# Retention, convolution and latent attention on one core: latent scaling inside the second query unit, and the shared key's columns beside the retention values

## The chip, the core and the metric

The kernel runs on one core of a Trainium2 chip. The metric is the device time of one execution in microseconds, lower is better. A profiled execution gives, beside its time, a trace: when each engine worked, on what, and what released it after each wait. The engines are TensorE (PE in the trace; its weight loads are PEld), VectorE (DVE), ScalarE (ACT), GpSimd (POOL) and the sequencer of SyncE (SP), which issues most of the DMA transfers.

## The reference, cut to what matters

x is 1024 rows of 1024 features in float32. All projections of x come from one matrix; the shared rope key is 64 of its columns, the query and key-value latents are 384 and 256 of them.

```python
h = rmsnorm(x, norm_g)
u_conv, u_ret, u_q, u_kv, u_kr, u_gate = split(h @ w_in)
y_conv = conv_module(u_conv, ...)        # GLU, 31 taps over the rows, channel LayerNorm, swish
y_ret = retention_branch(u_ret, ...)     # 4 heads of 128, rope, two scans, per-head norm
y_mla = mla_branch(u_q, u_kv, u_kr, ...) # latents are rms-normed, then 8 heads; k_rope = rope(u_kr)
y = concatenate([y_conv, y_ret, y_mla]) * silu(u_gate)
return rmsnorm(x + y @ w_out, final_g)
```

The rms norm of a latent is a division of each row of x's 1024 by that row's own root mean square, and a weight per latent channel.

## The kernel before

Everything is kept transposed: features lie on the 128 partitions, the 1024 rows of x along the free axis, in two halves of 512. A float32 product is made of three TensorE passes (`mm3`, L175 to L177) over high and low parts, so every operand is split once: ACT copies the high part (`xH`, `wh`), DVE subtracts to get the low part (`xL`, `wl`; L61 is the helper `stt` through which all such DVE operations go, L64 the helper `tt` for products and sums of two tensors on DVE or POOL).

The projections run as 21 units of 256 output columns (`run_unit`). A unit has four quarters (t = 0, 1 for the columns' halves, h = 0, 1 for the rows' halves) of 24 matmuls of 512 columns each. Units 0 to 3 feed the convolution, 4 to 7 are gates, 8 to 10 the latents, 11, 12 and 13 key, query and values of the first two retention heads, 14 a gate, 15 to 17 the other two heads, 18 to 20 gates. The values (`run_v`) are made the other way round, rows on the partitions, with 192 matmuls of 256 columns. Unit 10 holds one half of latent columns and one half in which the shared key's 64 columns stand twice.

Beside the units run background pieces (`bg`, `tick`). The convolution's taps are 120 DVE operations on 128 x 1024 (`acc <- hp, cwh, acc`); `hp` are the padded inputs of its four channel blocks. When the last tap of a block is done, the blocks are summed into `cm` (three DVE operations), TensorE sums `cm` over the channels (L353, two matmuls with a matrix of ones), DVE subtracts the mean, squares are summed into `va`, and so on to `y_dram`.

A latent quarter is evicted by DVE into `ca` (times the row factor of x's norm), stored to `l_dram`, squared by ACT, and the squares are added up by POOL in `lss` (query) and `lsk` (key-value). `row_rsqrt` (L300 to L308) sums these over the partitions on TensorE, in eight matmuls of one column for each of the two, and writes the 1024 row factors to `lq_dram` and `lk_dram`. After unit 20, when the attention begins, `lat` loads each half of a latent from `l_dram`, multiplies it by the broadcast row factors on DVE (ten products in all), and splits it; two more products make the shared key's rope parts (`kr`).

Rope of retention (`ev_rope`, L435 to L437): three DVE products of PSUM with tables, then one POOL sum into `k` or `q`.

TensorE's order, and that of each other engine, is fixed when the kernel is built, by the framework's scheduler; each engine then takes its queue in order and waits at the first instruction whose inputs are missing. At the start, `load_x` brings x in eight tiles of 128 features, SP issues, ACT scales by x's norm weights (in `vec`, one load of all small vectors issued by POOL), and TensorE runs warm-up passes (L264) on a zero tile. At the end, `finish` stores eight row blocks in two halves each, all issued by SP.

## Time and profile before

| | |
|---|---|
| median of three runs | 1117.38 us (1113.78 to 1118.88) |
| the profiled execution | 1115.57 us, span 1113.8 us |
| mean granted TensorE clock | 0.995 |
| TensorE busy | 1095.9 us, 98% of the span |
| DVE busy | 725.0 us, 65% |
| ACT busy | 412.9 us, 37% |
| POOL busy | 148.9 us, 13% |
| chain that ended last | TensorE 94%, DVE 3%, ACT 1%, DMA 1% |

The span runs from the first to the last instruction; the execution's own time is some 1.8 us longer. A granted clock of 1.00 is 2.4 GHz, the lower level 1.2 GHz; a figure between is a mean over a stretch with both.

### The profile page before, as it was taken

How to read it: one execution, taken by the hardware profiler on the slowest of the kernel's cores; microseconds unless marked ns; L12 is line 12 of the kernel's file. 1: busy time of each engine (PE TensorE's matmuls, PEld its weight loads, DVE VectorE, ACT ScalarE, POOL GpSimd, SP SyncE). 2: the span in 40 equal slices, each digit the busy share in tenths (PEclk: the TensorE clock that was granted, in tenths of full speed). 3: DMA queues.
4: the chain of work that ended last, by engine and by line, in shares of the span. 5: the costliest groups of instructions: out<-in, count | busy, mean ns of one | idle time of the engine just before them, and what ended most of it. 6: DMA issues, size and time to landing. Idle time of an engine off the chain costs nothing.

```text
span 1113.8 us, 14294 instructions
## 1 busy us (share of the span) xinstructions
PE 1095.9 (98%) x5568; PEld 920.2 (83%) x5568; DVE 725.0 (65%) x1011; ACT 412.9 (37%) x741; POOL 148.9 (13%) x135
## 2 busy tenths in 40 slices
PE   9999999999999999999899999999999999999997
PEld 7888888887898899888688888888888877888886
DVE  7599999998747694846865565655555572535033
ACT  8211221121144134324654554554554462424022
POOL 0200000213302442020201101200110000001000
PEclk9999999999999999999999999999999999999999
DMA  7221233221263121226211101211111241835112
GB/s 272 95 64 60 86 103 115 85 87 47 94 210 103 49 76 58 101 79 237 89 36 50 56 34 50 62 34 45 53 55 30 57 142 38 309 97 184 44 45 107
DMA packets 45620, 101.33 MB, mean 91 GB/s; under 512 B 5616, under 2 KB 9568, under 8 KB 45552
## 3 DMA queue, kind: packets, MB, share of 16 engines
q1 hardware_dynamic: 45504, 100.35, 27.2%
q8 instruction: 43, 0.70, 0.3%
q14 instruction: 25, 0.20, 0.1%
q0 software_dynamic: 48, 0.08, 0.0%
HBM read 74.14 MB, written 24.17 MB: 88 GB/s over the span
## 4 chain that ended last, share of the span: by engine, by line
PE 94%; DVE 3%; ACT 1%; DMA 1%; issue 1%; SPq 0%; POOLq 0%; POOL 0%; DVEq 0%; ACTq 0%
PE ps L175 24%; PE ps L176 24%; PE ps L177 24%; PE ps L831 5%; PE ps L813 3%; PE ps L817 3%; PE ps L816 3%; PE ps L814 3%; PE ps L815 3%; PE ps L576 1%; PE ps L565 1%; PE ps L300 1%; PE ps L580 1%; PE ps L578 1%; DMA xh<-lq_dram 0%
## 5 line engine op out<-in xcount | busy, mean ns | idle before, releaser
L176 PE MATMUL ps<-xL,wh 128*128 128x512 f32 (+1 forms) x612 | 238.9, 391 | 0.1
L177 PE MATMUL ps<-xH,wl 128*128 128x512 f32 (+1 forms) x612 | 238.6, 390 | 0.0
L175 PE MATMUL ps<-xH,wh 128*128 128x512 f32 (+1 forms) x612 | 236.3, 393 | 1.7 <-ACT xH L139 1.2
L61 DVE SCALAR_TENSOR_TENSOR acc<-hp,cwh,acc 128x1024 f32<-128x1024 f32 x120 | 154.0, 1323 | 0.1
L175 PEld LDWEIGHTS ps<-xH,wh 128*128 128x128 f32 x612 | 115.1, 189 | 25.5 <-ACT xH L139 1.4
L176 PEld LDWEIGHTS ps<-xL,wh 128*128 128x128 f32 x612 | 115.4, 188 | 24.2 <-DVE xL L61 0.8
L177 PEld LDWEIGHTS ps<-xH,wl 128*128 128x128 f32 x612 | 115.3, 188 | 23.8 <-issue 0.2
L61 DVE SCALAR_TENSOR_TENSOR PL<-ps,PH 128x512 fp32r<-128x512 f32 x128 | 85.6, 684 | 53.0 <-ACT PH L833 52.8
L833 ACT CAST PH<-ps 128x512 fp32r<-128x512 f32 x128 | 73.0, 588 | 92.2 <-PE ps L831 91.6
L176 PE MATMUL ps<-woL,yh 128*128 128x512 f32 (+1 forms) x264 | 100.8, 385 | 0.0
L177 PE MATMUL ps<-woH,yl 128*128 128x512 f32 (+1 forms) x264 | 100.2, 386 | 0.0
L175 PE MATMUL ps<-woH,yh 128*128 128x512 f32 (+1 forms) x264 | 100.0, 386 | 0.0
L820 DVE TENSOR_REDUCE nm<-ps 128x1 f32<-128x1024 f32 x64 | 78.1, 1220 | 31.9 <-PE ps L817 31.2
L166 ACT CAST wh<-wraw 128x1024 fp32r<-128x1024 f32 x40 | 42.1, 1052 | 126.0 <-PE ps L176 116.5
L822 ACT ACTIVATE P<-ps,nm 128x1024 f32<-128x1024 f32 x64 | 71.7, 1120 | 26.6 <-DVE nm L820 24.2
L831 PE MATMUL ps<-ident,P 128*128 128x128 f32 x512 | 72.8, 273 | 0.0
L831 PEld LDWEIGHTS ps<-ident,P 128*128 128x128 f32 x512 | 61.4, 140 | 12.7 <-DVE PL L61 0.8
L61 DVE SCALAR_TENSOR_TENSOR wl<-wraw,wh 128x1024 fp32r<-128x1024 f32 (+2 forms) x45 | 54.3, 1207 | 7.0 <-ACT wh L166 6.1
L813 PE MATMUL ps<-kH,qH 128*128 128x512 f32 x128 | 54.9, 429 | 3.8 <-DVE qL L61 2.6
L176 PEld LDWEIGHTS ps<-woL,yh 128*128 128x128 f32 x264 | 49.7, 188 | 10.3
L177 PEld LDWEIGHTS ps<-woH,yl 128*128 128x128 f32 x264 | 49.6, 188 | 10.2
L175 PEld LDWEIGHTS ps<-woH,yh 128*128 128x128 f32 x264 | 49.7, 188 | 10.0
(292 smaller groups left out, 1984.9 us busy)
## 6 DMA issues: line engine op xcount, KB each, us to landing
wraw<-in_w_in_dram SPq DMA_DIRECT2D x40, 512.0 KB, 3.5
wor<-in_w_out_dram SPq DMA_DIRECT2D x16, 512.0 KB, 4.7
g_dram<-ga SPq DMA_DIRECT2D x29, 256.0 KB, 2.2
yr<-y_dram SPq DMA_DIRECT2D x18, 256.0 KB, 3.7
g<-g_dram SPq DMA_DIRECT2D x16, 256.0 KB, 3.4
rb<-rs_dram SPq DMA_DIRECT2D x16, 256.0 KB, 3.1
y_dram<-osb SPq DMA_DIRECT2D x16, 256.0 KB
z<-in_x_dram SPq DMA_DIRECT2D x8, 512.0 KB, 3.5
```

Of the source, the lines that this page charges most:

```text
L61: eng.scalar_tensor_tensor(o, a, s, b, op0=op0, op1=op1)
L166: act.copy(hi, t)
L175: pe.matmul(o, sh, mh, start=first, stop=False, skip_group_check=skip)
L176: pe.matmul(o, sh, ml, start=False, stop=False, skip_group_check=skip)
L177: pe.matmul(o, sl, mh, start=False, stop=last, skip_group_check=skip)
L813: pe.matmul(o, qh[:, ts], kh, start=True, stop=False)
L814: pe.matmul(o, qh[:, ts], kl, start=False, stop=False)
L815: pe.matmul(o, ql[:, ts], kh, start=False, stop=False)
L820: dve.tensor_reduce(nm, self.S, axis=AX.X, op=MAX, negate=True)
L822: act.activation(p, self.S, AF.Exp, bias=nm, accum_out=self.rs[:, t:t + 1])
L831: pe.transpose(o[:, c * P:(c + 1) * P], self.p[t][:, (4 * j + c) * P:(4 * j + c + 1) * P], ident)
L833: act.copy(ph, o)
```

## The change

Four edits are made together.

1. Unit 10 runs its first half only. The shared key's 64 columns of weights are put beside the 256 of unit 13 (`load_v_kr`), whose matmuls become 320 wide (`run_v_kr`); ACT evicts values and key. After unit 14's first quarter `kr_rows` transposes the key's eight blocks on TensorE, multiplies by the rope tables on DVE and stores the two parts to `n_dram`, with sixteen transfers of 32 rows.
2. The latents are scaled in unit 12: `scale_lat`, called after each of its quarters, loads a whole latent tile and the row factors stay on chip in `lss` and `lsk`. POOL multiplies and the product goes to `n_dram`. The tiles have the tag `hp`, the convolution's inputs. `lat` then loads the scaled tile and only splits it, and the products and four row loads after unit 20 are gone.
3. x's norm weights come in a tile of their own (`gx`), loaded by SP second; `vec` is loaded by POOL at the very start. The first weight pieces are issued by ACT. The warm-up has nine rounds in place of twelve.
4. One of the last two stores is issued by ACT.

```diff
+WK = UW + 64
...
-NWARM = 12
+NWARM = 9
...
+    n_dram = [tc.dram_tile([P, S], F32, name=f"n_dram{i}") for i in range(QT + KVT + 1)]
...
+    gx = mk(const, [P, KT], tag="gx")
+    pool.dma_start(vec, vecs)
...
-        g = vec[:, V_G + k:V_G + k + 1]
+        g = gx[:, k:k + 1]
         for i in range(n):
             c = slice(i * S // n, (i + 1) * S // n)
             sp.dma_start(tf[:, c], xT[k * P:(k + 1) * P, c])
             if k == 0 and i == 0:
-                pool.dma_start(vec, vecs)
+                sp.dma_start(gx, vecs[:, V_G:V_G + KT])
                 w0[0][2](0, 1)
...
         def piece(a, b):
-            sp.dma_start(t[:, a:b], w_in[u, g, :, a:b])
+            (act if b == 1 or (g == 0 and b == 2) else sp).dma_start(t[:, a:b], w_in[u, g, :, a:b])
...
-    def run_unit(u, w, ev, nxt, per, hook=None):
+    def load_v_kr():
+        tiles = []
+        for tag in ("wh", "wl"):
+            two = [mk(p1, [P, 4, UW], F32R, tag=tag, bufs=4).rearrange("p a b -> p (a b)") for _ in range(2)]
+            two.append(mk(cv, [P, S + 2 * HALO], F32R, tag="hp", bufs=4))
+            tiles.append([v[:, :3 * WK].rearrange("p (a b) -> p a b", a=3) for v in two])
+        tk = mk(cv, [P, HS], tag="ca", bufs=4).rearrange("p (a b) -> p a b", a=KT)
+        for g in range(2):
+            sp.dma_start(tk[:, 4 * g:4 * g + 4], w_in[10, g, :, :, P:P + 64])
+        raw = []
+        for g in range(2):
+            raw.append(mk(p1, [P, 4, UW], tag="wraw", bufs=2))
+            sp.dma_start(raw[g], w_in[13, g])
+        for a, b in ((0, 3), (3, 4), (4, 6), (6, 8)):
+            for c, r in ((slice(0, UW), raw[a // 4][:, a % 4:a % 4 + b - a]), (slice(UW, WK), tk[:, a:b])):
+                hi, lo = (v[a // 3][:, a % 3:a % 3 + b - a, c] for v in tiles)
+                act.copy(hi, r)
+                split_l(dve, lo, r, hi)
+        return [(tiles[0][k // 3][:, k % 3], tiles[1][k // 3][:, k % 3]) for k in range(KT)]
+
+    def run_unit(u, w, ev, nxt, per, hook=None, each=None, ts=(0, 1)):
         res = None
-        for t in range(2):
+        for t in ts:
...
-                    res = load_unit(nxt)
+                    res = load_v_kr() if nxt == 13 else load_unit(nxt)
                 ev(t, h, o)
+                if each is not None:
+                    each(2 * t + h)
...
     for u in range(8, 11):
-        wn = run_unit(u, wn, ev_lat(2 * (u - 8)), u + 1, 2)
+        wn = run_unit(u, wn, ev_lat(2 * (u - 8)), u + 1, 2, ts=(0, 1) if u < 10 else (0,))
     lq_dram = tc.dram_tile([S], F32, name="lq_dram")
     lk_dram = tc.dram_tile([S], F32, name="lk_dram")
-    for ss, n, d in ((lss, 384.0, lq_dram), (lsk, 256.0, lk_dram)):
-        row_rsqrt(ss, 1.0 / n, EPS, None, d)
+    rows = []
+    for ss, n, d, tag in ((lss, 384.0, lq_dram, "lss"), (lsk, 256.0, lk_dram, "lsk")):
+        rows.append(mk(cv, [P, S], tag=tag))
+        row_rsqrt(ss, 1.0 / n, EPS, rows[-1], d)
+
+    def hp_tile():
+        return mk(cv, [P, S + 2 * HALO], tag="hp", bufs=4)
+
+    def scale_lat(i):
+        t = hp_tile()[:, :S]
+        sp.dma_start(t, l_dram[i])
+        if i < 5:
+            k = rows[int(i >= QT)]
+        else:
+            k = hp_tile()[:, :S]
+            sp.dma_start(k, t_mla[2])
+        tt(pool, t, t, k, MUL)
+        sp.dma_start(n_dram[i], t)
...
+    def run_v_kr(w, vN, per):
+        kn = mk(cv, [P, HS], tag="ca", bufs=4)
+        res = None
+        for st in range(NCH):
+            o = ps_main()
+            for k in range(KT):
+                mm3(o[:, :WK], xH[k][:, st * P:(st + 1) * P], xL[k][:, st * P:(st + 1) * P],
+                    w[k][0], w[k][1], k == 0, k == KT - 1)
+            if st == 0:
+                res = load_unit(14)
+            act.activation(vN[:, st, :], o[:, :UW], AF.Identity, scale=rcol[:, st:st + 1])
+            act.activation(kn[:, st * 64:(st + 1) * 64], o[:, UW:WK], AF.Identity, scale=rcol[:, st:st + 1])
+            if st % 2:
+                tick(per)
+        return res, kn
+
+    def kr_rows(kn):
+        for h in range(2):
+            o = ps_bg()
+            for j in range(4):
+                n = 4 * h + j
+                pe.transpose(o[:64, j * P:(j + 1) * P], kn[:, n * 64:(n + 1) * 64], ident)
+            tk, a = (hp_tile()[:64, :S].rearrange("p (c q) -> p c q", c=2) for _ in range(2))
+            hs = slice(h * HS, (h + 1) * HS)
+            for r, c, s0 in ((0, 0, 0), (32, 0, 32), (0, 1, 96), (32, 1, 64)):
+                sp.dma_start(tk[r:r + 32, c], t_mla[2][s0:s0 + 32, hs])
+            for c in range(2):
+                dve.tensor_tensor(a[:, c], o[:64], tk[:, c], op=MUL)
+            for r, c, s0 in ((0, 0, 0), (32, 0, 32), (0, 1, 96), (32, 1, 64)):
+                sp.dma_start(n_dram[5][s0:s0 + 32, hs], a[r:r + 32, c])
...
+    lat_at = {12: {0: (3, 4), 1: (0,), 2: (1,), 3: (2,)}}
     wn = run_unit(11, wn, ev_rope(kT[0], tr0, tmp0), 12, 3)
-    wn = run_unit(12, wn, ev_rope(qT[0], tr0, tmp0), 13, 3)
-    wn = run_v(13, wn, 14, vN[0], 3)
-    wn = run_unit(14, wn, ev_gate_t(8), 15, 6)
+    wn = run_unit(12, wn, ev_rope(qT[0], tr0, tmp0), 13, 3, each=lambda q: [scale_lat(i) for i in lat_at[12][q]])
+    wn, kn = run_v_kr(wn, vN[0], 3)
+    wn = run_unit(14, wn, ev_gate_t(8), 15, 6, lambda: kr_rows(kn))
...
-    def lat_rows(h):
-        rows[1, h] = row_bc(fin, "rb", lk_dram, h)
-        rows[0, h] = row_bc(wt, "xh", lq_dram, h)
...
-        sp.dma_start(t, l_dram[i][:, half(h)])
+        sp.dma_start(t, n_dram[i][:, half(h)])
         g = vec[:, V_QG + i:V_QG + i + 1]
-        tt(dve, t, t, rows[int(i >= QT), h], MUL)
         act.activation(lH[i][:, half(h)], t, AF.Identity, scale=g)
...
-        t, tk = mk(lx, [P, HS], tag="kr", bufs=2), mk(fin, [P, HS], tag="g" if h else "osb", bufs=2)
-        sp.dma_start(t, l_dram[5][:, half(h)])
-        sp.dma_start(tk, t_mla[2][:, half(h)])
-        tt(dve, t, t, tk, MUL)
+        t = mk(lx, [P, HS], tag="kr", bufs=2)
+        sp.dma_start(t, n_dram[5][:, half(h)])
         krt.append(t)
...
-            sp.dma_start(out[st * P:(st + 1) * P, half(c)], z[:, half(c)])
+            (act if st == 7 and c == 0 else sp).dma_start(out[st * P:(st + 1) * P, half(c)], z[:, half(c)])
```

Line numbers in the new kernel are a few higher (`tt` is L65, `stt` L62, `mm3` L179 to L181, the sums over the partitions L326, the cm matmul L379). The scheduler gives new orders in which the instructions stand.

POOL, from the end of unit 10 through unit 12, before (`k` and `q` are rope sums of units 11 and 12):

```order
L302 TENSOR_TENSOR rrc_1850<-rrc_1850,epsc_104 128x8
L302 TENSOR_TENSOR rrc_1866<-rrc_1866,epsc_104 128x8
L64 TENSOR_TENSOR k_1882<-ca_1928,ca_1929 128x512
L64 TENSOR_TENSOR k_1882<-ca_1962,ca_1963 128x512
L64 TENSOR_TENSOR k_1882<-ca_2001,ca_2002 128x512
L64 TENSOR_TENSOR k_1882<-ca_2042,ca_2043 128x512
L64 TENSOR_TENSOR q_1883<-ca_2095,ca_2096 128x512
L64 TENSOR_TENSOR q_1883<-ca_2149,ca_2150 128x512
```

And the same place now (`hp` are the latents that are scaled):

```order
L65 TENSOR_TENSOR k_1831<-ca_1911,ca_1912 128x512
L65 TENSOR_TENSOR k_1831<-ca_1945,ca_1946 128x512
L65 TENSOR_TENSOR hp_2059<-hp_2059,lsk_1813 128x1024
L65 TENSOR_TENSOR k_1831<-ca_1981,ca_1982 128x512
L65 TENSOR_TENSOR q_1832<-ca_2053,ca_2054 128x512
L65 TENSOR_TENSOR hp_2063<-hp_2063,lsk_1813 128x1024
L65 TENSOR_TENSOR hp_2106<-hp_2106,lss_1795 128x1024
L65 TENSOR_TENSOR q_1832<-ca_2100,ca_2101 128x512
L65 TENSOR_TENSOR hp_2166<-hp_2166,lss_1795 128x1024
L65 TENSOR_TENSOR hp_2212<-hp_2212,lss_1795 128x1024
```

Five products of twice the width stand among the rope sums of units 11 and 12.

TensorE at the end of unit 10 (`ps_1818` is its last quarter) and the start of unit 11, before:

```order
L176 MATMUL ps_1818<-xL_127,wh_1601 128x512
L177 MATMUL ps_1818<-xH_119,wl_1602 128x512
L300 MATMUL ps_1851<-ones_107,lss_1428 128x1 x8
L300 MATMUL ps_1867<-ones_107,lsk_1429 128x1 x8
L175 MATMUL ps_1891<-xH_112,wh_1735 128x512
```

And now:

```order
L180 MATMUL ps_1760<-xL_135,wh_1606 128x512
L181 MATMUL ps_1760<-xH_127,wl_1607 128x512
L326 MATMUL ps_1797<-ones_115,lss_1433 128x1 x8
L179 MATMUL ps_1840<-xH_120,wh_1740 128x512
L180 MATMUL ps_1840<-xL_128,wh_1740 128x512
L181 MATMUL ps_1840<-xH_120,wl_1741 128x512
L179 MATMUL ps_1840<-xH_121,wh_1740 128x512
L180 MATMUL ps_1840<-xL_129,wh_1740 128x512
L326 MATMUL ps_1815<-ones_115,lsk_1434 128x1 x4
L181 MATMUL ps_1840<-xH_121,wl_1741 128x512
```

The one-column sums of lsk have moved into unit 11, four of them here and four a quarter later.

TensorE at the convolution's sum over channels, before, in the third quarter of unit 11 (`ps_1976`):

```order
L175 MATMUL ps_1976<-xH_118,wh_1741 128x512
L353 MATMUL ps_1968<-cm_428,ones_107 128x512
L176 MATMUL ps_1976<-xL_126,wh_1741 128x512
L177 MATMUL ps_1976<-xH_118,wl_1742 128x512
L175 MATMUL ps_1976<-xH_119,wh_1741 128x512
L176 MATMUL ps_1976<-xL_127,wh_1741 128x512
L177 MATMUL ps_1976<-xH_119,wl_1742 128x512
L353 MATMUL ps_2015<-cm_428,ones_107 128x512
```

And now, in the third quarter of unit 12 (`ps_2135`):

```order
L179 MATMUL ps_2135<-xH_126,wh_1871 128x512
L180 MATMUL ps_2135<-xL_134,wh_1871 128x512
L379 MATMUL ps_1952<-cm_433,ones_115 128x512
L379 MATMUL ps_2067<-cm_433,ones_115 128x512
L181 MATMUL ps_2135<-xH_126,wl_1872 128x512
```

The two matmuls on cm stand four quarters of a unit further on in the row of units, twenty matmuls into a quarter.

## Rows read from the trace of the kernel before

**Rows 1.** The page's first part: busy time, share of the span, instructions.

```profile
PE 1095.9 (98%) x5568; PEld 920.2 (83%) x5568; DVE 725.0 (65%) x1011; ACT 412.9 (37%) x741; POOL 148.9 (13%) x135
```

**Rows 2.** Timeline of TensorE, units 10 and 13: start us, us, engine, line, out<-in.

```profile
225.29 0.39 PE L175 MATMUL ps<-xH,wh 128*128 128x512 f32 x1
...
230.73 0.39 PE L175 MATMUL ps<-xH,wh 128*128 128x512 f32 x1
...
302.76 0.28 PE L176 MATMUL ps<-wl,xH 128*128 128x256 f32 x1
...
308.52 0.28 PE L176 MATMUL ps<-wl,xH 128*128 128x256 f32 x1
```

**Rows 3.** Timeline of TensorE: one-column sums at the start and after unit 10.

```profile
36.32 1.84 PE L300 MATMUL ps<-ones,cm 128*128 128x1 f32 x16
...
249.10 1.84 PE L300 MATMUL ps<-ones,lss 128*128 128x1 f32 x16
250.80 1.93 PE L300 MATMUL ps<-ones,lsk 128*128 128x1 f32 x16
...
253.60 0.57 PE L176 MATMUL ps<-xL,wh 128*128 128x512 f32 x1
...
257.24 0.40 PE L176 MATMUL ps<-xL,wh 128*128 128x512 f32 x1
```

**Rows 4.** Windows: length; busy PE, PEld, DVE, ACT, POOL; PEclk; DMA share; GB/s.

```profile
38.00:43.00 5.00, 5.00 (x24) 4.14 (x24) 0.91 (x6) 0.00 (x0) 1.67 (x1) 1.00 0.03 10
253.00:258.00 5.00, 5.00 (x17) 3.91 (x16) 4.96 (x7) 0.00 (x0) 4.33 (x2) 0.66 0.47 157
```

**Rows 5.** Timeline of TensorE, start; in brackets idle before, and its releaser.

```profile
9.91 1.20 PE L175 MATMUL ps<-xH,wh 128*128 128x512 f32 x4 [1.18 <-ACT xH L139]
```

**Rows 6.** Windows, the attention's first tiles.

```profile
525.00:545.00 20.00, 15.85 (x62) 10.88 (x61) 18.04 (x30) 12.36 (x23) 3.84 (x3) 0.91 0.50 172
```

**Rows 7.** Timeline of TensorE, the attention's first scores.

```profile
539.92 0.50 PE L813 MATMUL ps<-kH,qH 128*128 128x512 f32 x1 [2.62 <-DVE qL L61]
```

**Rows 8.** Groups of DVE from 511 to 545: busy us, mean ns | idle before.

```profile
L64 DVE TENSOR_TENSOR lt<-lt,xh 128x512 f32<-128x512 f32 x4 | 2.6, 682 | 0.0
```

**Rows 9.** Timeline of SP's issues, the rotated query.

```profile
535.40 2.50 SPq L762 DMA_DIRECT2D xs<-xr  x4
```

**Rows 10.** Timeline of the last microseconds, SP's issues.

```profile
1110.01 0.81 SPq L1046 DMA_DIRECT2D out_dram<-z  x2
```

**Rows 11.** Timeline of DVE, from unit 10 to unit 15.

```profile
234.15 4.70 DVE L61 SCALAR_TENSOR_TENSOR acc<-hp,cwh,acc 128x1024 f32<-128x1024 f32 x3
...
245.79 2.47 DVE L61 SCALAR_TENSOR_TENSOR acc<-hp,cwh,acc 128x1024 f32<-128x1024 f32 x2
...
260.04 0.69 DVE L435 TENSOR_TENSOR ca<-ps,xn 128x512 f32<-128x512 f32 x1 [0.21 <-POOL rrc L302]
...
262.17 2.41 DVE L61 SCALAR_TENSOR_TENSOR acc<-hp,cwh,acc 128x1024 f32<-128x1024 f32 x1
264.61 1.22 DVE L64 TENSOR_TENSOR cm<-cm,acc 128x1024 f32<-128x1024 f32 x1
...
287.79 2.38 DVE L64 TENSOR_TENSOR va<-va,cb 128x512 f32<-128x512 f32 x2
...
343.22 0.15 DVE L507 TENSOR_SCALAR kd<-kd 128x8 f32<-128x8 f32 x1
```

**Rows 12.** Timeline of POOL: the rope tables, and a sum of unit 11.

```profile
49.92 4.79 POOL L64 TENSOR_TENSOR xn<-xn,rbc 128x1024 f32<-128x1024 f32 x2 [9.73 <-DMA rbc<-r_dram]
...
262.21 1.28 POOL L64 TENSOR_TENSOR k<-ca,ca 128x512 f32<-128x512 f32 x1 [2.20 <-DVE ca L437]
```

**Rows 13.** Timeline of TensorE: cm, va, the first decayed values' product.

```profile
269.79 1.02 PE L353 MATMUL ps<-cm,ones 128*128 128x512 f32 x2
...
291.33 0.95 PE L300 MATMUL ps<-ones,va 128*128 128x1 f32 x8
...
353.82 0.23 PE L175 MATMUL ps<-w,w 128*128 128x128 f32 x1
```

More of the change, by code (lines that the diff above doesn't have):

```diff
@@ L105, in body @@
     pool.memset(eps_c, -0.5)
-    cwh = mk(const, [P, 144], tag="cwh")[:, :NC_CONV * CONV_K]
+    cwh = mk(const, [P, 136], tag="cwh")[:, :NC_CONV * CONV_K]
     ones = mk(const, [P, P], tag="ones")
@@ L403, in ev @@
             sp.dma_start(l_dram[i][:, hs], a)
-            if i < 5:
-                dst = lss if i < QT else lsk
-                if i in (0, QT):
-                    act.activation(dst[:, hs], a, AF.Square)
-                else:
-                    sq = mk(cv, [P, HS], tag="cb", bufs=2)
-                    act.activation(sq, a, AF.Square)
-                    tt(pool, dst[:, hs], dst[:, hs], sq, ADD)
+            dst = lss if i < QT else lsk
+            if i in (0, QT):
+                act.activation(dst[:, hs], a, AF.Square)
+            else:
+                sq = mk(cv, [P, HS], tag="cb", bufs=2)
+                act.activation(sq, a, AF.Square)
+                tt(pool, dst[:, hs], dst[:, hs], sq, ADD)
         return ev
     for u in range(8, 11):
-        wn = run_unit(u, wn, ev_lat(2 * (u - 8)), u + 1, 2)
+        wn = run_unit(u, wn, ev_lat(2 * (u - 8)), u + 1, 2, ts=(0, 1) if u < 10 else (0,))
     lq_dram = tc.dram_tile([S], F32, name="lq_dram")
     lk_dram = tc.dram_tile([S], F32, name="lk_dram")
-    for ss, n, d in ((lss, 384.0, lq_dram), (lsk, 256.0, lk_dram)):
-        row_rsqrt(ss, 1.0 / n, EPS, None, d)
+    rows = []
[9 more added lines that the diff above has]
+            k = rows[int(i >= QT)]
+        else:
+            k = hp_tile()[:, :S]
+            sp.dma_start(k, t_mla[2])
+        tt(pool, t, t, k, MUL)
+        sp.dma_start(n_dram[i], t)
     def trig(pl, tag):
@@ L663, in half @@
         return slice(i * HS, (i + 1) * HS)
-    def row_bc(pl, tag, d, h):
-        t = mk(pl, [P, HS], tag=tag)
-        sp.dma_start(t, d[half(h)].rearrange("(o s) -> o s", o=1).to_broadcast([P, HS]))
-        return t
-    krt, rows = [], {}
-    def lat_rows(h):
-        rows[1, h] = row_bc(fin, "rb", lk_dram, h)
-        rows[0, h] = row_bc(wt, "xh", lq_dram, h)
+    krt = []
     def lat(i, h):
@@ L686, in body @@
     LT = [(lx, "lt", LTB)] * LTB + [(fin, "osb", 2), (fin, "g", 2)] * 2
-    lat_rows(0)
     lat(3, 0)
@@ L866, in body @@
     g_r(0, 0)
-    lat_rows(1)
     lat(3, 1)
```

## Prediction

> **What bounds the kernel now.** I read the engines' busy times first: TensorE is busy for 98% of the span [rows 1], so time can only go in three ways: fewer or narrower matmuls, fewer waits of TensorE, or less time at the lower clock. Then I read TensorE's timeline for the price of a matmul. Two starts 24 matmuls of 512 columns apart differ by 5.44 us, or 0.2267 us each; two starts 48 matmuls of 256 columns apart differ by 5.76 us, or 0.120 us each [rows 2]. A straight line through both gives 0.0133 us plus 0.000417 us a column, hence 0.1467 us for 320 columns, a width that the trace does not have. Last I looked for the stretches in which TensorE waits or runs slow near the lines touched: the sums of squares after unit 10, the attention's first tiles, the start, and the end.
>
> **The change part by part.**
>
> *Matmuls.* Unit 10's second half held 48 matmuls of 512 columns: 48 x 0.2267 = 10.9 us go. Unit 13's 192 matmuls grow from 256 to 320 columns: 192 x 0.0267 = 5.1 us come. Eight transposes come, each no dearer than a 256-column matmul: at most 1.0 us, I take 0.9. Net **-4.9**, all of it on the path, since TensorE is the path. Bounds: if the 320-column step costs as a 512-column one in proportion (0.142) or has the line's offset twice (0.160), the net moves from -5.8 to -2.3.
>
> *The clock after the sums.* Before, 16 one-column passes for lss and 16 for lsk stand together [rows 3]. Behind them nine intervals of 512-column matmuls take 3.64 us instead of 2.04, and the granted clock of that stretch is 0.66, which is 1.2 GHz for a part of it and 2.4 GHz for the rest [rows 3, 4]. Behind the one set of 16 at 36.32 the clock stays at 1.00 [rows 3, 4]. The change puts six full matmuls after lss, and splits lsk in two. I take the whole dip as gone, **-1.6** (0 to -1.6).
>
> *Start.* TensorE waits 1.18 us for the first 512-column x tile at 9.91 [rows 5]. The norm weights now come in a small load of their own, and two weight pieces are issued by ACT; but the bytes ahead of that tile are the same. I take **-0.4** (0 to -1.2). Three fewer rounds of warm-up cost nothing unless the clock falls there: the real matmuls follow within the same microseconds.
>
> *Attention's first tiles.* In 525 to 545 us TensorE is busy for 15.85 of 20, so 4.15 are idle, and the mean granted clock is 0.91 [rows 6]: 20 x 0.09 = 1.8 us more at 1.2 GHz. Some 6 us are to be had. The biggest wait, 2.62 us, is for qL of DVE [rows 7], and DVE is full there: 18.0 of 20 us [rows 6]. The change takes ten products of 0.68 us for the latents (four of them are in [rows 8]) and two for the key off DVE, about 8 us, and six loads of 256 KB. What stays is the chain of the rotated query: four small copies issued one after another in 2.50 us [rows 9] and three POOL products behind. So not all 6 come back: I take **-4** (-2 to -6).
>
> *End.* One of the two last stores, which SP issues in 0.81 us [rows 10], goes to ACT: **-0.3** (0 to -0.4). These gains make -11.2.
>
> *The price: conv's end on DVE.* The scaling now stands in unit 12 as five POOL products of 128x1024, and conv's last taps lie there too. What POOL does to DVE the trace shows: two taps alone take 2.47 us, one beside POOL's k product (1.28 us long) 2.41 [rows 11, 12]. So a 512-wide POOL product costs DVE about 1.2 us where DVE has two SBUF inputs, and a 1024-wide one, 2.4 us long [rows 12], about 2.4. The Trainium skill, "GPSIMD Engine Reference", section 1 (Specifications), says that POOL's SBUF interfaces are shared with VectorE and collide with DVE instructions of two SBUF inputs, and section 4.1 sends elementwise tile work to VectorE. By that rule the products give DVE nothing back, and the time is the forecast's; were the ports separate, it would be the first rival's. The 2.41 us row agrees with the rule.
>
> DVE works from 234.15 without a real gap until cm is done at 264.61 + 1.22 = 265.8 [rows 11]: 31.7 us. TensorE asks for cm at 269.79 [rows 13], 4 us later. In the new order the same stretch ends four quarters further on, two of them in place of the two that unit 10 lost. It loses two evictions of 0.7 (-1.4), and gains four more rope groups of 2.1 each (the one from 260.04 to 262.17 [rows 11]; +8.5), the weight splits for unit 13 (two of 1.2 and small ones; +3.2), four more rope products of POOL beside taps or splits (4 x 1.2 = +4.8), and one or two scalings on POOL (+2.4 to +4.8). That makes 49.2 to 51.6 us, so cm is done at 283.4 to 285.8. TensorE gets there sooner: unit 10 ends one half (10.9) before 249.1, at 238.2; then the sums 3.5, unit 11 21.8, and 15.4 into unit 12: about 279.0. The wait is 4.4 to 6.8; some products will meet DVE on PSUM inputs, which costs nothing, so I take **+5** (0 to +9, the latter with a third scaling ahead of cm). The matmuls behind it stand in TensorE's one queue and all wait. A wait that long is followed in this trace by the lower clock (the 2.62 us wait lies in the stretch of 0.91 [rows 6, 7]): **+1.7** (0 to 2).
>
> *What cm passes on.* The squares' sums (va) come next. DVE's last va products end at 287.79 + 2.38 = 290.2, and TensorE's matmul is at 291.33 [rows 11, 13], 1.2 us of margin; between cm and va DVE gets more in its way than TensorE does: **+1** (0 to 3.8). Then the tail: kd is ready at 343.37 [rows 11], 52.0 us after that va matmul, and one ACT product and one split later the first matmul on it could start, some 53.3; it is at 353.82 [rows 13], 62.5 after. In the new order fewer matmuls stand between the two (144 of 512, 122 of 320 instead of 167 of 512, 192 of 256): about 53. The margin of 9 is spent to zero: **+1** (0 to 9, from sixteen more small copies on SP at 2.50/4 = 0.6 each).
>
> Sum: -4.9 - 1.6 - 0.4 - 4 - 0.3 + 5 + 1.7 + 1 + 1 = **-2.5** against the profiled execution's 1115.57: 1113.1. The median shown, 1117.38, is 1.8 higher, the lowest run 1.8 lower; I go a little up from the sum, to 1113.5. A measurement of this kernel tells about 0.5% (5.6 us) from no change.
>
> **The rivals.**
>
> *No wait at cm.* POOL's products fall beside rope, whose inputs are in PSUM, and DVE keeps its 42.0 us without contention: cm is ready at 234.15 + 42.0 = 276.2 + what k products add, at most 279. Then only the gains stand: 1115.57 - 11.2 = 1104.4. For it: TensorE's order was given a place for cm well behind DVE's bare work. Against it: the 2.41 us tap.
>
> *The latents' gain is small.* If the copies for the rotated query and their POOL products set the time by themselves, the wait for qL is only renamed, and -4 becomes -1: 1116. Against it: the copies start from DVE's rows, which come earlier with 8 us taken off.
>
> *The tail blocks (slower).* The sixteen copies of 32 rows go on SP's queue between the loads and stores of conv's normalisation, and the tables for the next heads wait for that tail. If all sixteen stand ahead, 16 x 0.6 = 9.6 us, the first product with the decayed values waits about 9 instead of 1, with 1.7 of slow clock behind it: 1113.1 + 8 + 1.7 = 1122.8. It decides from the point where the tail grows by more than the zero margin above; under 4 us it stays inside my range. For it: SP's queue is in order. Against it: half of the copies are behind the stores that matter, or DMA is nearly idle there.
>
> *The change does not separate the sums.* If the lower clock follows anyway and the five 1024-wide products cost nothing more, 1115.1: inside the forecast's range.
>
> **How the numbers follow.** Forecast, a wait at cm of some 5 us: 0.44, between 1109 and 1118. No wait: 0.30, 1102 to 1107. Small gain at the latents: 0.10. Tail: 0.10. Clock unchanged: 0.06. The range must reach to the no-wait case and short of the tail: 1103 to 1121. Faster by over 0.5%: the 0.30 and a quarter of the forecast, 0.41. Slower: the tail and a little of the small-gain case, 0.12. Within 0.5%: the rest, 0.47.
>
> **What would show it.** In the changed kernel's profile: starts of unit 13's matmuls 0.147 apart; no stretch at half clock behind lss; taps of over 2 us beside POOL's hp products; an idle of 4 to 7 us of TensorE before the cm matmuls, released by DVE's cm, and the lower clock behind it; in the attention's first 20 us no wait for qL and less than 2 us idle; the first product with kd with a wait near zero. I am wrong if cm is there before TensorE (then 1104), if the idle near the latents stays at 4, or if the first matmul on the decayed values waits more than 4 us.

## The result

The changed kernel takes 1124.53 us (median of 6 runs, 1122.53 to 1126.21), the kernel before 1118.01 us beside it (1113.78 to 1119.00): a ratio of 1.0068, 95% interval 1.0051 to 1.0086. It is slower by 6.5 us between the medians and 7.6 by the ratio. The prediction was 1113.5, with a range to 1121 and a chance of 0.12 for this side. One later execution, of the kernel `ends`, took 1916.6 us at a mean granted clock of 0.67 and is left out of that kernel's ratio.

The page of the profiled execution (1126.21 us, span 1124.4, the slowest of the six) shows at once where to look: TensorE's busy time is that of [rows 1], but the chain that ended last, TensorE's for 94% before, is now TensorE's for 83% only.

```profile
PE 1095.6 (97%) x5522; PEld 920.4 (82%) x5522; DVE 729.8 (65%) x1007; ACT 415.4 (37%) x755; POOL 165.3 (15%) x140
...
PE 83%; DVE 8%; DMA 4%; issue 3%; ACT 1%; SPq 0%; POOL 0%; POOLq 0%; DVEq 0%; ACTq 0%
```

TensorE's timeline gives the waits (in brackets: idle before, released by). "The decayed values" are the retention values times the decay factors kd, in unit 15; the first matmul on them reads the tiles `w,w`. A later `w,w`, in unit 17, waits too. These waits and those for cm and va are new; that for qL has shrunk from [rows 7], and one for QA, the rotated query, has come.

```profile
281.94 3.39 PE L379 MATMUL ps<-cm,ones 128*128 128x512 f32 x4 [2.85 <-DVE cm L65]
...
301.90 1.02 PE L326 MATMUL ps<-ones,va 128*128 128x1 f32 x8 [1.11 <-DVE va L65]
...
361.03 0.48 PE L179 MATMUL ps<-w,w 128*128 128x128 f32 x1 [4.48 <-ACT w L608]
...
420.61 0.39 PE L180 MATMUL ps<-w,w 128*128 128x256 f32 x1 [1.82 <-DVE w L62]
...
547.89 0.50 PE L873 MATMUL ps<-kH,qH 128*128 128x512 f32 x1 [0.96 <-DVE qL L62]
...
553.85 0.50 PE L876 MATMUL ps<-K,QA 128*128 128x512 f32 x1 [2.00 <-ACT QA L835]
```

Behind these waits the granted clock (third number from the end) is low for a while. 5 us at 0.66 lose 1.7 us, 25 us at 0.86 lose 3.5, and 25 us at 0.93 lose 1.75.

```profile
280.00:285.00 5.00, 3.06 (x5) 1.44 (x5) 4.81 (x6) 0.22 (x1) 5.00 (x3) 0.66 0.35 112
350.00:375.00 25.00, 20.52 (x97) 17.38 (x97) 22.05 (x51) 8.34 (x24) 10.41 (x7) 0.86 0.20 72
400.00:425.00 25.00, 23.18 (x146) 21.28 (x145) 24.40 (x44) 7.87 (x17) 11.43 (x9) 0.93 0.21 65
550.00:575.00 25.00, 23.00 (x116) 19.06 (x115) 15.47 (x21) 15.29 (x28) 6.17 (x5) 0.93 0.11 28
```

From one same matmul in both, 581.91 before and 592.07 after, the two profiles are 10.2 us apart, and at the end 10.6, so nearly all of it happens earlier. The parts: start -0.4, matmuls -4.9, the dip of [rows 3] -1.6, cm 2.85 and its clock 1.7, va 1.1, the decayed values 4.5 and their clock 3.5, the later `w,w` 1.8 and its clock 1.75. That is +10.3; the attention's first tiles gave nothing in this execution (before, 4.15 idle and 1.8 of clock; after, waits of 1.32, 0.96 and 2.00 us and 1.75 of clock: some 6.0 each).

```profile
581.91 0.50 PE L175 MATMUL ps<-lH,whk 128*128 128x512 f32 x1 [1.01 <-DVE kL L61]
```

```profile
592.07 0.50 PE L179 MATMUL ps<-lH,whk 128*128 128x512 f32 x1 [1.01 <-DVE kL L62]
```

Two causes for the lateness offered themselves. The first is POOL's products beside DVE. In the changed kernel's DVE and POOL timelines a weight split of 768 columns takes 3.15 us beside a product of 2.86, and later one of 1024 columns 3.44 beside two that take 6.06 (an operation of that width on two SBUF inputs takes 1.22 in [rows 11]):

```profile
265.86 3.15 DVE L62 SCALAR_TENSOR_TENSOR wl<-wraw,wh 128x768 fp32r<-128x768 f32 x1
...
291.57 3.44 DVE L62 SCALAR_TENSOR_TENSOR wl<-wraw,wh 128x1024 fp32r<-128x1024 f32 x1
```

```profile
265.32 2.86 POOL L65 TENSOR_TENSOR hp<-hp,lsk 128x1024 f32<-128x1024 f32 x1 [0.47 <-DMA lsk<-lk_dram]
...
291.21 6.06 POOL L65 TENSOR_TENSOR hp<-hp,lss 128x1024 f32<-128x1024 f32 x2 [3.52 <-DMA hp<-l_dram]
```

The second is the transfers behind unit 14. Followed back from the wait at 361.03, the chain (start, us, what) runs through loads, one of which takes 7.05 us and one 6.76, with two issues of the small stores (L532) in between:

```profile
320.66 4.80 DMA cb<-g_dram
...
329.51 7.05 DMA cb<-g_dram
...
337.70 3.90 DMA cb<-g_dram
...
343.53 0.45 SPq L532
344.02 0.54 SPq L532
...
345.91 6.76 DMA w<-in_t_idx_dram
```

### The profile page after: what moved, and what is told of

Same layout as the page of the kernel before. It is cut to its first block, busy times and chain, and to the rows that moved or that the text cites. A ratio compares the mean times of both kernels' runs of the same rounds, so it can differ in the third digit from the quotient of the medians.

```text
span 1124.4 us, 14278 instructions
## 1 busy us (share of the span) xinstructions
PE 1095.6 (97%) x5522; PEld 920.4 (82%) x5522; DVE 729.8 (65%) x1007; ACT 415.4 (37%) x755; POOL 165.3 (15%) x140
## 4 chain that ended last, share of the span: by engine, by line
PE 83%; DVE 8%; DMA 4%; issue 3%; ACT 1%; SPq 0%; POOL 0%; POOLq 0%; DVEq 0%; ACTq 0%
PE ps L179 20%; PE ps L180 20%; PE ps L181 20%; PE ps L891 4%; PE ps L873 3%; PE ps L876 3%; PE ps L877 3%; PE ps L874 3%; PE ps L875 3%; DMA cb<-g_dram 1%; DVE acc L62 1%; DVE w L62 1%; DMA g_dram<-xr 1%; DVE wl L62 1%; PE ps L649 1%
## 5 line engine op out<-in xcount | busy, mean ns | idle before, releaser
L180 PE MATMUL ps<-xL,wh 128*128 128x512 f32 (+1 forms) x596 | 232.0, 390 | 0.6 <-DVE xL L62 0.5
L181 PE MATMUL ps<-xH,wl 128*128 128x512 f32 (+1 forms) x596 | 232.4, 391 | 0.0
L179 PE MATMUL ps<-xH,wh 128*128 128x512 f32 (+1 forms) x596 | 229.3, 392 | 2.8 <-DVE xr L62 1.3
L62 DVE SCALAR_TENSOR_TENSOR acc<-hp,cwh,acc 128x1024 f32<-128x1024 f32 x120 | 154.3, 1324 | 0.1
L179 PEld LDWEIGHTS ps<-xH,wh 128*128 128x128 f32 x596 | 111.8, 188 | 26.1 <-DVE xr L62 1.7
L180 PEld LDWEIGHTS ps<-xL,wh 128*128 128x128 f32 x596 | 112.3, 188 | 23.5 <-DVE xL L62 1.2
L181 PEld LDWEIGHTS ps<-xH,wl 128*128 128x128 f32 x596 | 112.3, 188 | 23.3 <-issue 0.5
L62 DVE SCALAR_TENSOR_TENSOR PL<-ps,PH 128x512 fp32r<-128x512 f32 x128 | 85.5, 685 | 52.3 <-ACT PH L893 52.2
L181 PE MATMUL ps<-woH,yl 128*128 128x512 f32 (+1 forms) x264 | 100.2, 386 | 0.0
L179 PE MATMUL ps<-woH,yh 128*128 128x512 f32 (+1 forms) x264 | 100.0, 386 | 0.0
L170 ACT CAST wh<-wraw 128x1024 fp32r<-128x1024 f32 x38 | 39.8, 1052 | 107.2 <-PE ps L180 99.8
L62 DVE SCALAR_TENSOR_TENSOR wl<-wraw,wh 128x1024 fp32r<-128x1024 f32 (+3 forms) x46 | 60.9, 1327 | 4.8 <-ACT wh L170 4.7
L65 POOL TENSOR_TENSOR g<-g,rb 128x512 f32<-128x512 f32 x16 | 21.0, 1314 | 254.7 <-DMA rb<-rs_dram 209.5
L180 PEld LDWEIGHTS ps<-woL,yh 128*128 128x128 f32 x264 | 49.7, 188 | 10.2
L179 PEld LDWEIGHTS ps<-woH,yh 128*128 128x128 f32 x264 | 49.7, 188 | 10.1
L181 PEld LDWEIGHTS ps<-woH,yl 128*128 128x128 f32 x264 | 49.6, 188 | 10.1
```

The lines of the kernel that those rows point to most:

```text
L62: eng.scalar_tensor_tensor(o, a, s, b, op0=op0, op1=op1)
L170: act.copy(hi, t)
L179: pe.matmul(o, sh, mh, start=first, stop=False, skip_group_check=skip)
L180: pe.matmul(o, sh, ml, start=False, stop=False, skip_group_check=skip)
L181: pe.matmul(o, sl, mh, start=False, stop=last, skip_group_check=skip)
```

## The experiments

Theory A says that both causes act, on a way that the shared key's new place has made shorter for TensorE; B, that POOL's products cause all; C, that the shorter way alone does. Ratios are to the kernel before, run beside each; an expectation in microseconds that was written against another session's median is judged by the ratio.

| kernel | median us | before beside it | ratio (95%) |
|---|---|---|---|
| no_scale | 1119.26 | 1115.44 | 1.0029 (1.0014 to 1.0044) |
| no_merge | 1113.94 | 1115.44 | 0.9984 (0.9970 to 0.9997) |
| thin_products | 1116.26 | 1115.44 | 1.0015 (0.9993 to 1.0037) |
| few_copies | 1120.74 | 1115.44 | 1.0037 (1.0016 to 1.0057) |
| wide_key | 1118.23 | 1115.28 | 1.0020 (0.9997 to 1.0043) |
| late_wide | 1128.80 | 1115.28 | 1.0112 (1.0075 to 1.0149) |
| ends | 1116.02 | 1115.28 | 0.9999 (0.9981 to 1.0018) |
| split | 1115.30 | 1115.28 | 0.9996 (0.9980 to 1.0012) |
| wide_dve | 1122.31 | 1116.90 | 1.0045 (1.0026 to 1.0064) |
| nm_dve | 1112.85 | 1116.90 | 0.9965 (0.9949 to 0.9981) |
| thin_wide | 1111.02 | 1116.90 | 0.9958 (0.9945 to 0.9971) |
| no_scale_wide | 1116.35 | 1116.90 | 0.9998 (0.9984 to 1.0013) |

A difference of two of these ratios, worked out from their intervals, is known to some 0.27%, or 3 us, to either side.

### Undoing one part

**no_scale**: the latents' scaling goes back to DVE in the attention.

```diff
-    wn = run_unit(12, ..., each=lambda q: [scale_lat(i) for i in lat_at[12][q]])
+    wn = run_unit(12, ...)
...
+        tt(dve, t, t, rows[int(i >= QT), h], MUL)
```

> The changed kernel, with the latents scaled on DVE in the attention as before; the shared key stays beside the values, and TensorE's order at cm is that of the changed kernel. Theory A (two causes: POOL's products make cm and va late, and the sixteen small copies behind unit 14 together with a shorter way for TensorE make the decayed values late): the waits for cm (2.85 us) and va (1.11 us) and the 1.7 us at half clock behind them are gone, the wait for the decayed values stays at 4 us or more; about 1119. Rival B (POOL's products are the cause of all, the tail's delay is handed on from cm): no wait over 1 us before unit 16; about 1111. Rival C (the shorter way alone, not lateness of DVE): cm waits still over 2 us; 1123.

The cm wait is 0.84 us and va's is gone. The decayed values wait 2.34, half as long as in the changed kernel and not 4: part of that wait had been handed on from cm, as B says, part had not. (Some loads and stores of the latents are gone here too; thin_products keeps them.) In the attention the wait for qL is 3.49 us, longer than in [rows 7].

```profile
353.89 0.33 PE L179 MATMUL ps<-w,w 128*128 128x128 f32 x1 [2.34 <-ACT w L606]
...
540.64 0.79 PE L882 MATMUL ps<-kH,qH 128*128 128x512 f32 x1 [3.49 <-DVE qL L62]
```

**no_merge**: the key's columns go back to unit 10.

```diff
-        wn = run_unit(u, wn, ev_lat(2 * (u - 8)), u + 1, 2, ts=(0, 1) if u < 10 else (0,))
+        wn = run_unit(u, wn, ev_lat(2 * (u - 8)), u + 1, 2)
...
-    wn, kn = run_v_kr(wn, vN[0], 3)
-    wn = run_unit(14, wn, ev_gate_t(8), 15, 6, lambda: kr_rows(kn))
+    wn = run_v(13, wn, 14, vN[0], 3)
+    wn = run_unit(14, wn, ev_gate_t(8), 15, 6)
```

> The changed kernel with unit 10 in full and the key's columns there, as before; the latents are still scaled by POOL in unit 12. TensorE's order at the sums and at cm is that of the kernel before. Theory A: cm is not late (the products come behind it), the va matmul waits up to 3 us, the decayed values don't wait, since TensorE's way there has its old length; the attention's first tiles give 1 to 2 us back; about 1117. Rival B (POOL's products alone cost the time): va and the decayed values wait 3 us and more; about 1122.

As A expected, a little better: va waits 1.02, the decayed values not at all. The attention's first tiles do give what the prediction promised: 2.36 us idle in 25 and a clock of 1.00 (last but two), in place of 4.15 idle in 20 and 0.91 [rows 6]. In the same run TensorE stands 3.7 us behind the kernel before when it comes to the key's rows and 0.2 behind it at the matmul of 581.91, so the scaling outside the attention is worth 3.5 us there.

```profile
293.37 1.05 PE L326 MATMUL ps<-ones,va 128*128 128x1 f32 x8 [1.02 <-DVE va L65]
...
540.39 0.50 PE L877 MATMUL ps<-kH,qH 128*128 128x512 f32 x1 [1.30 <-DVE qL L62]
```

```profile
525.00:550.00 25.00, 22.64 (x99) 17.24 (x99) 17.41 (x26) 14.81 (x27) 3.85 (x3) 1.00 0.50 170
```

### Taking one cost away

**thin_products**: the products stay, 8 columns wide.

```diff
-        tt(pool, t, t, k, MUL)
+        tt(pool, t[:, :8], t[:, :8], k[:, :8], MUL)
```

> The changed kernel with each of POOL's five products done on the first 8 of its 1024 columns only, so that the other columns of the latents go unscaled; all transfers stay. Theory A: DVE's operations beside them go back to their own length, the waits for cm and va and the half clock behind (2.85, 1.11, 1.7) go, the decayed values still wait 3 to 5 us; about 1119. Rival B: the wait for the decayed values goes too; about 1113. Rival D (not the port but the loads and stores of the latents): nothing changes; 1124.

The changed kernel stood at 1.0068, this one at 1.0015: 0.53%, 5.9 us, are the work of POOL's products on DVE, and rival D falls, since all loads and stores are there. The 768-wide split, which still meets a rope sum on POOL, takes 2.05 us in place of 3.15. cm waits 0.79, va does not wait, the decayed values 2.57, much as in no_scale: about 2 of the 4.5 us were handed on, 2.5 are another cause's, and B falls.

```profile
265.08 2.05 DVE L62 SCALAR_TENSOR_TENSOR wl<-wraw,wh 128x768 fp32r<-128x768 f32 x1
```

**few_copies**: eight copies of 64 rows.

```diff
-            for r, c, s0 in ((0, 0, 0), (32, 0, 32), (0, 1, 96), (32, 1, 64)):
-                sp.dma_start(tk[r:r + 32, c], t_mla[2][s0:s0 + 32, hs])
+            for c in range(2):
+                sp.dma_start(tk[:, c], t_mla[2][64 * c:64 * c + 64, hs])
```

> The changed kernel with eight copies of 64 rows in place of the sixteen of 32 behind unit 14, so that the halves of the shared key's rows are stored in a wrong place. Theory A: half of SP's issues there go, 5 us of SP's queue; the wait for the decayed values falls from 4.48 to 1 to 3 us; 1119 to 1122. Rival C (the shorter way alone): the wait stays at 4 to 5; 1124.

The ratio falls by 0.31%, 3.5 us, as A expected, though with 3 us to either side. The trace does not show how. The wait of the decayed values falls to 0.98, while cm still waits 2.85 and va 1.99, but not because the values come sooner: the last operation on kd starts 55.9 us after the second va matmuls (360.87 - 305.02), and 56.2 in the changed kernel (360.28 - 304.04). It is TensorE that comes later, 55.6 us after those matmuls in place of 52.5: from 300 to 325 us its granted clock is 0.86 here and 1.00 there, and 25 us at 0.86 lose 3.5. So this profile decides nothing between A and C. In the changed kernel:

```profile
304.04 1.02 PE L326 MATMUL ps<-ones,va 128*128 128x1 f32 x8
...
360.28 0.15 DVE L580 TENSOR_SCALAR kd<-kd 128x8 f32<-128x8 f32 x1
...
300.00:325.00 25.00, 23.89 (x162) 23.17 (x161) 9.74 (x12) 12.32 (x23) 2.85 (x2) 1.00 0.38 122
```

And in few_copies:

```profile
305.02 1.37 PE L326 MATMUL ps<-ones,va 128*128 128x1 f32 x8
...
360.87 0.15 DVE L580 TENSOR_SCALAR kd<-kd 128x8 f32<-128x8 f32 x1
...
361.61 0.33 PE L179 MATMUL ps<-w,w 128*128 128x128 f32 x1 [0.98 <-ACT w L608]
...
300.00:325.00 25.00, 23.01 (x140) 22.65 (x139) 10.30 (x12) 9.49 (x20) 2.69 (x2) 0.86 0.21 75
```

**wide_key**: the same with a whole output. ACT writes the key's 64 columns and their swapped halves side by side, the transposes give all 128 rows, and one load and one store of 128 rows serve each half. With that go one DVE product of 128 rows for two of 64, three ACT writes for one, and a change of buffers (the key in an `hp` tile).

```diff
-        kn = mk(cv, [P, HS], tag="ca", bufs=4)
+        kn = hp_tile()[:, :S]
...
+            for d0, s0, w0_ in ((0, 0, 64), (64, 32, 32), (96, 0, 32)):
+                act.activation(kn[:, st * P + d0:st * P + d0 + w0_], o[:, UW + s0:UW + s0 + w0_], AF.Identity, scale=rcol[:, st:st + 1])
...
+            sp.dma_start(tk, t_mla[2][:, hs])
+            dve.tensor_tensor(a, o, tk, op=MUL)
+            sp.dma_start(n_dram[5][:, hs], a)
```

> The changed kernel with the key kept as 128 columns a block (ACT writes the swapped halves), so that four transfers of 128 rows stand behind unit 14 in place of sixteen of 32; the output is whole. Theory A (the small copies lengthen the way to the decayed values, beside POOL's products that make DVE late): the wait for the decayed values falls from 4.48 to 1 or 2 us, cm still waits 2.85: 3 to 5 us under the changed kernel, about 1120. Rival C (only TensorE's shorter way): the wait stays, 1124.

1.0020 in place of 1.0068, 5.4 us for four transfers instead of sixteen of the same bytes. The decayed values don't wait at all, although cm waits 2.96 and va 1.93. Here they do come sooner: the last operation on kd starts 52.6 us after the second va matmuls (357.06 - 304.44), 3.6 less than in the changed kernel. The table that starts them is issued 40.3 us after those matmuls (41.9 in the changed kernel, 304.04 to 345.91), and lands after 3.54 us in place of 6.76. TensorE is a little late too, 53.9 us (granted clock 0.93 from 300 to 325); at the changed kernel's 52.5 some 0.9 us of the wait would be left, an estimate from these rows.

```profile
304.44 1.27 PE L326 MATMUL ps<-ones,va 128*128 128x1 f32 x8
...
344.75 3.54 DMA w<-in_t_idx_dram
...
357.06 0.16 DVE L578 TENSOR_SCALAR kd<-kd 128x8 f32<-128x8 f32 x1
```

**thin_wide**: both taken away, in the kernel of wide_key.

```diff
-        tt(pool, t, t, k, MUL)
+        tt(pool, t[:, :8], t[:, :8], k[:, :8], MUL)
```

> The kernel of wide_key with the five POOL products on 8 of 1024 columns, which leaves the other columns unscaled: both suspected causes are taken away, TensorE's shorter way stays. Theory A: cm waits 0.8, va and the decayed values not at all or under 0.5 us, and the 4.9 us of matmuls stay in the time; about 5 to 6 us under the kernel before. Rival C (the shorter way alone makes waits): the decayed values still wait 2 us and more; at most 2 us under the kernel before.

0.9958, 4.7 us under the kernel before (a range of 3.2 to 6.1): theory A's figure was 5 to 6. From wide_key that is 0.62%, 6.9 us for the products; from thin_products it is 0.57%, 6.4 us for the copies. So each cause costs about the same with the other and without it (copies 5.4 and 6.4, products 5.9 and 6.9, each to some 3), and together they make up the 1.1% between the changed kernel and this one. cm waits 0.68, the decayed values not at all, though TensorE's way to them is as short as ever (52.4 us after the second va matmuls): C falls. Here the 768-wide split meets no product at all but a thin one and takes 0.95 us:

```profile
266.03 0.95 DVE L62 SCALAR_TENSOR_TENSOR wl<-wraw,wh 128x768 fp32r<-128x768 f32 x1
```

Two waits stay on TensorE:

```profile
410.25 0.39 PE L180 MATMUL ps<-w,w 128*128 128x256 f32 x1 [1.83 <-DVE w L62]
...
542.78 0.50 PE L874 MATMUL ps<-K,QA 128*128 128x512 f32 x1 [1.84 <-ACT QA L833]
```

The first of them is there in every kernel with the key in its new place (1.25 to 1.83 us; wide_key has one of 0.48 before it), and in none without. The lower clock stands behind it in five of the nine profiles (waits of 1.61 to 1.83) and not in the other four (1.25 and 1.27). What in the new order makes it is not settled.

### Looking for a version that keeps the gains

**late_wide**: wide_key, with the products asked for in unit 13. In the other kernels the scheduler draws them forward; here the key holds one of the four `hp` tiles, and they stand behind unit 12's rope sums.

```diff
-    lat_at = {12: {0: (3, 4), 1: (0,), 2: (1,), 3: (2,)}}
+    lat_at = {2: (3,), 3: (4,), 4: (0,), 5: (1,), 6: (2,)}
```

> The kernel of wide_key, with the five POOL products asked for in unit 13 in place of unit 12; in POOL's order they then stand behind the last rope sum of unit 12, that is behind cm and va, where DVE waits for the row factors. Theory A: cm waits under 1 us and va not at all, the decayed values 0 to 2 us; of the 6.9 us of matmuls, sums and start, 4 to 5 stay, and 1 to 2 in the attention: about 5 us under the kernel before. Rival C: cm still waits over 2 us and the decayed values over 3; at the kernel before or above.

A miss by far: 1.0112 (four runs), where 5 us less than before were expected. cm waits 0.79, as A said; but the loads and stores of the latents now lie on SP's queue among those of conv's normalisation, and the table for the decayed values is issued 49.7 us after the va matmul (302.90) instead of 41.9. I had moved the products, and not asked what their transfers would meet. va's wait of 1.99 fits a product of POOL that stands beside DVE's va products at 298.35.

```profile
365.18 0.48 PE L179 MATMUL ps<-w,w 128*128 128x128 f32 x1 [5.94 <-ACT w L607]
```

```profile
352.63 0.33 SPq L568 DMA_DIRECT2D w<-in_t_idx_dram  x1
```

**no_scale_wide**: wide_key with the latents scaled in the attention as before.

```diff
-        tt(pool, t, t, k, MUL)      # scale_lat, with its calls
+        tt(dve, t, t, rows[int(i >= QT), h], MUL)      # lat
```

> The kernel of wide_key with the latents scaled on DVE in the attention as before. Theory A: up to unit 16 as thin_wide, that is without waits over 1 us; at the attention's first scores the wait for qL of 3.5 us as in no_scale, with the half clock behind it; 2 to 4 us under the kernel before. Rival C: the decayed values wait 2 us as in no_scale; at or above the kernel before.

Up to unit 16 as expected: cm 0.68, nothing for the decayed values. The wait for qL is 3.48, and the ratio is 0.9998, not 2 to 4 us under. TensorE stands 2.2 us ahead of the kernel before at the key's rows and 0.9 ahead at 581.91: part of what is saved before the attention is lost again in its first tiles, where TensorE waits for DVE.

**wide_dve** and **nm_dve**: the products on DVE, in wide_key and in no_merge.

```diff
-        tt(pool, t, t, k, MUL)
+        tt(dve, t, t, k, MUL)
```

> The kernel of wide_key with the five products done by DVE in unit 12 in place of POOL. The port shared by POOL and DVE is not in the plan that sets TensorE's order (the order with POOL's full products is that with thin ones), a product on DVE is: the cm matmuls move 13 places further on. Theory A: DVE spends 5 x 1.2 us on them in place of 5 x 2.4 lost beside POOL, cm waits under 1 us in place of 2.96 and va under 0.5 in place of 1.93; 4 to 5 us under wide_key, some 1 to 2 under the kernel before. Rival: the products cost DVE the same on either engine, cm and va wait as in wide_key; at wide_key.

> The kernel of no_merge (unit 10 in full, latents scaled in unit 12) with the products on DVE. Theory A: va's wait of 1.02 us and the half clock behind it go, the attention keeps its 3.5 us; 3 to 4 us under the kernel before. Rival: DVE is late for va all the same; at no_merge or above.

In wide_dve cm waits 0.59 as said, but va 2.29, and the median is 1122.31 (1.0045): a miss. Its profiled execution is the shortest of its ten runs, so the rows don't show where the others lose more; that stays open. nm_dve has the lowest ratio of the kernels with a whole output: 1112.85, 0.9965 (0.9949 to 0.9981), 3.9 us under the kernel before. no_merge, at 0.9984, is under it too, and the two intervals overlap. The time of nm_dve is as expected, but the reason is not shown: va waits 1.06 and the decayed values 1.97 in the profiled execution, which at 1116.26 is the longest of its runs.

```profile
282.21 1.98 PE L379 MATMUL ps<-cm,ones 128*128 128x512 f32 x4 [0.59 <-DVE cm L65]
301.64 1.02 PE L326 MATMUL ps<-ones,va 128*128 128x1 f32 x8 [2.29 <-DVE va L65]
```

```profile
296.43 1.05 PE L326 MATMUL ps<-ones,va 128*128 128x1 f32 x8 [1.06 <-DVE va L65]
...
356.55 0.33 PE L179 MATMUL ps<-w,w 128*128 128x128 f32 x1 [1.97 <-ACT w L610]
```

### Two small terms

**ends**: the third and fourth edit on the kernel before.

```diff
-                pool.dma_start(vec, vecs)
+                sp.dma_start(gx, vecs[:, V_G:V_G + KT])
...
-            sp.dma_start(t[:, a:b], w_in[u, g, :, a:b])
+            (act if b == 1 or (g == 0 and b == 2) else sp).dma_start(t[:, a:b], w_in[u, g, :, a:b])
```

> The kernel before with the third and fourth edit alone (norm weights in a tile of their own, first weights and one last store issued by ACT, nine rounds of warm-up). By the prediction's terms -0.4 and -0.3: 0.7 us under the kernel before. Rival: the first x tiles are bound by the bytes ahead of them, nothing changes at the start; -0.3 or none.

0.9999, with an interval of some 2 us to either side: the predicted -0.7 can be neither seen nor excluded. The first x tile's wait is 0.65 us in this profile (1.18 in [rows 5]), but 1.25 in thin_products, which has the same start, and 1.73 in split, which has that of before: it changes from run to run by as much as the edit was to bring.

**split**: the sums of lsk a quarter later.

```diff
-    for ss, n, d in ((lss, 384.0, lq_dram), (lsk, 256.0, lk_dram)):
-        row_rsqrt(ss, 1.0 / n, EPS, None, d)
+    row_rsqrt(lss, 1.0 / 384.0, EPS, None, lq_dram)
...
+    wn = run_unit(11, ..., lambda: row_rsqrt(lsk, 1.0 / 256.0, EPS, None, lk_dram))
```

> The kernel before with the sums of lsk asked for a quarter later, so that 24 full matmuls stand between them and those of lss. If the two sets side by side bring the lower clock: the granted clock behind each set is 1.00, and the time falls by 1.6 us. Rival: the lower clock follows the second set all the same, or one of the sets; no change.

0.9996, with an interval that holds both nothing and the 1.6 us. The profiles say more. Take that of ends first. It has the two sets side by side, as before, and no dip:

```profile
248.62 1.84 PE L302 MATMUL ps<-ones,lss 128*128 128x1 f32 x16
250.32 1.93 PE L302 MATMUL ps<-ones,lsk 128*128 128x1 f32 x16
```

```profile
250.00:275.00 25.00, 25.00 (x119) 20.14 (x119) 23.05 (x29) 3.96 (x7) 10.21 (x5) 1.00 0.15 52
```

But of the four profiles with the two sets side by side three have the dip: before (0.93 in that stretch), no_merge and nm_dve:

```profile
250.00:275.00 25.00, 25.00 (x103) 20.11 (x104) 19.91 (x24) 2.38 (x5) 16.97 (x7) 0.86 0.52 191
```

```profile
250.00:275.00 25.00, 25.00 (x111) 19.91 (x111) 23.26 (x25) 1.18 (x4) 11.05 (x4) 0.93 0.58 194
```

Of the ten with the sets apart (split, the changed kernel and its eight relatives that keep the key beside the values), none has: the clock is 1.00 from 236 to 276 us in all of them. So in the profiles the dip goes with the order, but it is no constant price: with the sets side by side it costs 0, 1.7, 1.7 and 3.5 us. The 1.6 us are about their mean; the time of split is too coarse to confirm them.

## Why the prediction was wrong, point by point

**Matmuls, -4.9: right.** Unit 13's starts 24 matmuls apart differ by 3.51 us, 0.1463 each, against 0.1467. (The 4.7 us of thin_wide lie near it, but hold the sums, the start, the latents and the waits that stay as well, so they are no measure of this term.)

```profile
291.55 0.30 PE L179 MATMUL ps<-wh,xH 128*128 128x320 f32 x1
...
295.06 0.31 PE L179 MATMUL ps<-wh,xH 128*128 128x320 f32 x1
```

**cm, +5 and 1.7: the mechanism right, the size too big.** TensorE came at 279.1 (281.94 - 2.85; predicted 279.0), cm at 281.9 (predicted 283.4 to 285.8); the wait was 2.85, the clock 1.7. Of the wait, 0.8 is not the products': thin_products has 0.79 without them. One product stood beside a split ahead of cm, and cost it 2.2 us (3.15 in place of 0.95), where 2.4 had been reckoned from the 2.41 us row; so the price was right, and the first rival, no wait at cm, is out. What the sum gave no place is the part handed on behind va: by thin_products the products cost 5.9 us in all, to some 3; in the profiles they make about 2 of wait at cm, 1.7 of its clock, 1.1 at va and 2 at the decayed values.

**va, +1: right** (1.11).

**The tail, +1: the step that failed.** The profile has 8.0 here, 4.5 of waiting and 3.5 of clock; the sign that the text named for being wrong, a wait of more than 4 us, came. The text worked out that the margin of 9 us was spent to zero, named the sixteen copies, left a longer tail to a rival with a chance of 0.10, and then took the low end of 0 to 9 for a tail of unchanged length. TensorE came as predicted, 52.5 us after the second va matmuls (about 53). But kd's last operation, 51.9 after them before (343.22 - 291.33), came at 56.2. With margin zero that is paid in full, and the clock behind it. Taken from wide_key, thin_products and thin_wide (52.6, 54.3 and 51.5), the copies lengthen the tail by 2.8 to 3.6 us and the products by 1.1 to 2.0; in the time the copies cost 5.4 and 6.4.

The rival's 1122.8 lies near the measured time, but in part by luck. It reckoned 9.6 us of SP's issues ahead of the table; the table is issued only 1.2 us later behind the va matmuls than before (41.9 against 331.99 - 291.33 = 40.7), and what differs more is its landing (6.76 us, and 3.54 with four transfers). Its reason against itself, that DMA is nearly idle there, was wrong: the DMA share from 325 to 350 was 0.51 before and is 0.80 after. The share alone does not make the wait, though: in wide_key it is 0.90. And the forecast's case and this rival were not two cases but came together: the delays of both add up.

**Unit 17's `w,w`, not foreseen:** 1.8 us and 1.75 of clock in this profile; in the nine with the key beside the values 1.25 to 1.83, five of them with the clock behind it.

**The latents, -4: right in no_merge (3.5), lost in the changed kernel's profile.** There the wait for qL falls from 2.62 to 0.96, but that for QA, which the text named as what stays, comes to 2.00 with the lower clock behind it. In few_copies, thin_products, wide_key and thin_wide QA waits 1.8 to 2.0 as well, but the clock stays at 1.00: there waits of 3.5 to 4.1 us stand against some 6 before, a gain of about 2.

**The sums, -1.6: there in this profile, not a constant.** No dip stands behind the sums in the changed kernel (five full matmuls behind lss, not six), as predicted; but one execution's dip was taken for that of all (0 to 3.5 us in four profiles), and the time of split neither shows nor excludes it.

**Start and end, -0.7: below what can be seen.**

Taken together, for the two profiled executions (their 10.6 us hold more of the lower clock than the 6.5 between the medians):

| term | predicted | in the profiles |
|---|---|---|
| matmuls, sums, start | -6.9 | -6.9 |
| latents | -4 | 0 |
| behind 592.07, the end with it | -0.3 | +0.4 |
| cm and its clock | +6.7 | +4.55 |
| va | +1 | +1.1 |
| tail and its clock | +1 | +8.0 |
| unit 17's `w,w` and its clock | none | +3.55 |
| sum | -2.5 | +10.7 |

## What to carry to other kernels

When a change shortens the bottleneck's way to a wait, work out the margin that is left at every wait behind it; where it is near zero, all delays on the other side add up there, so price them together and not as rivals of each other. When a wait shrinks in an experiment, look which side moved: in few_copies it was the engine that waits, not what it waits for. Work given to GpSimd is not free for VectorE while that reads two SBUF inputs, and this scheduler does not move TensorE's order for it: the order was the same with the full products as with thin ones. Many small transfers on a queue that a chain of loads runs through cost more than their bytes: four of 128 rows for sixteen of 32, with the smaller changes that go with them, were worth 5.4 us here, to some 3.
